# One product with the meta values for four frame tiles, in one PSUM bank, in a two-layer streaming encoder

## The chip, the cores and the metric

The kernel runs on one core of a Trainium2 chip. The metric is the device time of one execution in microseconds (us). The kernel before took 1335.31 us, the median of 3 runs (1331.56, 1336.21 and 1335.31).

Five engines work side by side, each on its own list of instructions: TensorE (PE, with its weight loads shown apart as PEld), VectorE (DVE), ScalarE (ACT), GpSimd (POOL), and SyncE (SP), which issues the transfers. Products are written to PSUM, which has eight banks of 512 float32 values on each of 128 partitions; ACT and DVE read them out of there.

## The reference, cut to what matters

Two layers over 592 tokens: 512 frames, 16 meta tokens ahead of them, and 64 sample tokens of another stream. Each layer makes one wide input projection, a recurrent branch, a differential attention branch with 8 heads, and two output projections. The attention of one head over the prompt, which is what the change touches, is:

```
s = einsum('bqhcd,bkhcd->bhcqk', q, k) * HEAD_DIM ** -0.5      # two maps, c = 0, 1
s = where(mask, s, -inf)                    # frames see the meta tokens and chunks up to their own
p = softmax(s, axis=-1)
attn = p[:, :, 0] - lam * p[:, :, 1]
o = einsum('bhqk,bkhe->bqhe', attn, v)      # v has 128 columns per head
o = rms_norm(o, subln_w) * (1 - lam_init)   # over the 128 columns of a head
```

The queries of the frames are four tiles of 128. Tile i sees the 16 meta tokens and the frame tiles 0 to i, so its output is `attn_meta(i) @ v_meta + sum over j <= i of attn(i, j) @ v(j)`. Sample and meta queries are a fifth tile of 80 rows.

## The kernel before, in words

**Projections.** Nearly all of PE's work is `dense` (L208): a block of 128 output columns over 592 tokens, in two halves of up to 296 tokens. Each half is 24 products (8 slices of the contraction, and for each hi*hi, hi*lo and lo*hi of a float32r split). The weights come by DMA (`stg`), ACT copies the high part (`wh`, L156) and DVE or POOL subtracts the low part (`wl`, L161). POOL does it in the step after three halves, (Z, 0), (Z, 1) and (A, 0) (`POOL_LO`, L43).

**What sets the order.** The order is written out by hand: no scheduler moves anything. For each of 8 heads the blocks A, B, V and Z (queries, keys, values, gate) are projected in turn. After each half `dense` runs, in this order: the deferred instructions (`flush`), the evacuation of the half, one `step()` of every active generator, and the next pieces of `wl` and `wh`. `head_steps` is such a generator; it begins after a head's Z block and does the attention of the head piecemeal between the halves of the next heads' blocks. So the four frame tiles of head h get their products while head h+1 is projected: tiles 3 and 2 after the second half of V (the V step below), tiles 1 and 0 after the first half of Z (the first Z step), the sample tile after the second half of Z (the second Z step), and the root of the norm on POOL after the first half of the A block that follows (L618 on).

**The products (`PV_step`).** For a frame tile, L541 multiplies PM, the transposed meta probabilities of all four tiles (16 meta rows of tile i at partitions 32i), with `vm[:, i]`, in which only the 16 rows of tile i are filled; L543 adds one product for each frame tile j up to i. All of them are float32 with 128 moving columns. Tiles 3 and 1 go to the bank `po`, tiles 2 and 0 to the bank `pt`. ACT copies each output to `oraw` (L550) and squares it with a running sum into a column of `ss` (L552). Each float32 product shows as two PE records, one for each of two weight loads; they are called passes here.

**What follows on the same engines.** In each step the same head's successor also runs its scores: in the V step and in the Z steps PE goes on with L476 and L479 into `pss`, DVE takes the row maximum (`nm`, L506), ACT the exponentials (`P`, L509), and then the next `wh`. At the next `flush` DVE combines the two maps (L483, L484 and `AT`, L489), and behind that stands the evacuation of the Z half (`zt` on DVE, L756, and `zg` on ACT, L757).

Of the kernel before, what the change touches and what calls it, by code (L numbers as in the profile page):

```python
# [22 lines left out]
FT = mybir.dt.float32  # L23
# [3 lines left out]
AF = mybir.ActivationFunctionType  # L27
# [60 lines left out]
def tile_kernel(ctx, tc, I, O):  # L88
    nc = tc.nc
    V, S, P, PE, SY = nc.vector, nc.scalar, nc.gpsimd, nc.tensor, nc.sync  # L90
    ctx.enter_context(tc.manual_schedule())

    def pool(name, **kw):
        return tc.tile_pool(name=name, bufs=1, reuse_waits="tile", **kw)
# [8 lines left out]
    def blk(name, dt=FT, w=T):  # L103

        return ar.tile([128, w], dt, name=name, tag="blk", bufs=ARENA)
# [4 lines left out]
    def ps_t():  # L110
        return ps.tile([128, 512], FT, name="pt")
# [4 lines left out]
    def ps_o():  # L116
        return ps.tile([128, 512], FT, name="po")
# [276 lines left out]
    po = ps_o()  # L394
# [15 lines left out]
    for k in range(KT):  # L410
# [6 lines left out]
        sq = acc0 if k == 0 else blk("sq")  # L417
# [3 lines left out]
        for n in range(2):  # L421
            for i, (a, b) in enumerate(((0, hwh), (0, hwl), (1, hwh))):
                for hf, (c0, m) in enumerate(ALL):
                    PE.matmul(banks[n][hf][:, :m], wt[n][a][:, k], b[k][:, c0:c0 + m], start=(k == 0 and i == 0),
                              stop=(k == KT - 1 and i == 2))
# [10 lines left out]
    def head_steps(l, h, at, shared, QF, KF, kcv, vT, gate, oa):  # L436
        AM, qlz, vt, vm = shared
# [30 lines left out]
        ss = at.tile([128, 5], FT, name="ss", bufs=2)  # L468
        P.memset(Z, 1.0)
        P.memset(ss, 1.0)  # L470
        AT, PT, pcs = {}, {}, {}
# [56 lines left out]
        def T_sample():  # L528
# [4 lines left out]
            PT[4] = at.tile([128, 3, 80], FT, name="PT4")  # L533
            S.activation(PT[4].rearrange("p a b -> p (a b)"), pa[:, :240], AF.Copy)

        def PV_step(i, p):
            nq = 128 if i < 4 else 80
            if i < 4:
                j0 = i * (i + 1) // 2
                o = p[:, :128]  # L540
                PE.matmul(o, PM, vm[:, i], start=True, stop=False)  # L541
                for j in range(i + 1):
                    PE.matmul(o, PT[0][:, j0 + j], vt[:, j], start=False, stop=(j == i))  # L543
            else:
                t = PT[4]
                for j in range(2):
                    PE.matmul(p[:nq, :128], t[:, j], cv[:, j], start=(j == 0), stop=False)
                PE.matmul(p[:nq, :128], t[:, 2], vt[:, 4], start=False, stop=True)

            S.activation(oraw[:nq, i], p[:nq, :128], AF.Copy)  # L550
            sq = at.tile([128, 128], FT, name="sq")
            S.activation(sq[:nq], oraw[:nq, i], AF.Square, accum_out=ss[:nq, i:i + 1])  # L552

        build(0)
        yield
# [33 lines left out]
        PM = at.tile([128, 128], FT, name="PM")  # L589
# [13 lines left out]
        yield  # L603
        oraw = at.tile([128, 5, 128], FT, name="oraw")
        P.memset(oraw[64:, 4], 0.0)
        PV_step(3, ps_o())
        PV_step(2, ps_t())
        yield
        PV_step(1, ps_o())
        PV_step(0, ps_t())  # L610
        yield
        PV_step(4, ps_t())
        rz0 = at.tile([128, 5], FT, name="rz0", bufs=2)
# [25 lines left out]
        o = oa[h] = blk("oa")  # L639
# [9 lines left out]
    def head(l, h, at, shared, hw, oa, hook, after):  # L649
# [96 lines left out]
        def evac_zs(hf, *x):  # L746
            evac_z(hf, *x)
            if hf == 1:
                active.append(head_steps(l, h, at, shared, QK[0], QK[1], kcv, vT, lambda: zg, oa))
# [78 lines left out]
    for l in range(DEPTH):  # L828
# [6 lines left out]
        at = ats.enter_context(pool(f"at{l}"))  # L835
# [3 lines left out]
        vt = at.tile([128, 5, 128], FT, name="vt")  # L839
        vm = at.tile([128, 4, 128], FT, name="vm")  # L840
# [21 lines left out]
        for nm in order_rnn():  # L862
            j = int(nm[2:])
# [50 lines left out]
            if rp is None and not active:  # L914
# [5 lines left out]
                    lambda n, dt, i=i: rp.tile([128, T], dt, name=f"{n}{i}") for i in range(3)]))  # L920
# [248 lines left out]
```

## Time and profile before

| | |
|---|---|
| median of 3 runs | 1335.31 us |
| the profiled execution | 1332.49 us, of which the span is 1330.6 us |
| PE busy | 1311.8 us (99%), 9768 records |
| DVE, ACT, POOL busy | 969.5 (73%), 674.0 (51%), 370.8 us (28%) |
| granted PE clock | 0.998 of full speed |
| DMA | 179.06 MB, mean 135 GB/s |

The span is the time from the first to the last instruction of the profiled execution; the 1.9 us around it are start and end. A busy share of 99% says that PE has almost always something under way; the ends of its records are modelled and overlap, so what one product takes of PE's time is read from start to start in the timeline. ACT's and POOL's busy time lies beside PE's, and counts only where PE waits for what they make.

### The profile page before, as it was taken

Reading aid. Unit: us, or ns where it says so; the run is one execution under the profiler, and the core shown is the slowest. Engines: PE = TensorE matmul, PEld = TensorE weight load, DVE = VectorE, ACT = ScalarE, POOL = GpSimd, SP = SyncE. Lnnn points to the kernel's source line nnn. Section 1 sums busy time; section 2 is a strip of 40 time slices with the busy share of each in tenths; the row PEclk is TensorE's granted clock in tenths of the full one; section 3 lists DMA queues with packets and bytes.
Section 4 is the critical chain, followed back from the end, with each engine's and each line's share of the span. In section 5 each row is a group of like instructions: output and inputs, shape, how many; then the busy total and the mean of one; then the engine's idle time right before and its main releaser. Section 6 shows DMA issues by size and latency. Waiting matters only on the chain.

```text
span 1330.6 us, 26310 instructions
## 1 busy us (share of the span) xinstructions
PE 1311.8 (99%) x9768; PEld 1305.4 (98%) x9768; DVE 969.5 (73%) x2031; ACT 674.0 (51%) x1575; POOL 370.8 (28%) x736
## 2 busy tenths in 40 slices
PE   8999999999999999999999999999999999999997
PEld 8999999999999999999999999999999999999997
DVE  6998888875467886555568888888734789855566
ACT  5465555564236674423425555555642566653343
POOL 1324544442212331000212344444331144200011
PEclk9999999999999999999999999999999999999999
DMA  6557777775332221223543677777653222222254
GB/s 227 170 139 182 179 169 181 180 168 146 98 110 86 73 84 64 97 80 116 179 143 112 168 187 178 177 180 185 161 155 106 85 76 88 80 80 80 90 184 139
DMA packets 260575, 179.06 MB, mean 135 GB/s; under 512 B 177952, under 2 KB 222624, under 8 KB 260448
## 3 DMA queue, kind: packets, MB, share of 16 engines
q1 hardware_dynamic: 260016, 176.85, 47.5%
q8 instruction: 77, 1.26, 0.4%
q14 instruction: 50, 0.41, 0.1%
q10 hardware_dynamic: 432, 0.53, 0.1%
HBM read 132.37 MB, written 35.26 MB: 126 GB/s over the span
## 4 chain that ended last, share of the span: by engine, by line
PE 79%; issue 7%; POOL 5%; DVE 3%; DMA 3%; ACT 1%; SPq 1%; ACTq 0%; POOLq 0%; DVEq 0%
PE pd L208 68%; PE pss L476 2%; PE pss L479 2%; PE pss L789 2%; PE po L543 2%; DMA stg<-in_w_dram 1%; PE pss L208 1%; PE pt L543 1%; POOL wl L161 1%; DMA gw<-in_gw_dram 1%; POOL ny L276 1%; POOL na L271 1%; DMA kcv<-in_cache_dram 1%; PE pt L541 1%; PE po L541 0%
## 5 line engine op out<-in xcount | busy, mean ns | idle before, releaser
L208 PE MATMUL pd<-hwh,wl 128*128 128x296 f32 (+1 forms) x1968 | 587.9, 299 | 6.0 <-POOL wl L161 5.3
L208 PE MATMUL pd<-hwh,wh 128*128 128x296 f32 (+1 forms) x1968 | 589.0, 299 | 0.4 <-DVE xs L662 0.4
L208 PE MATMUL pd<-hwl,wh 128*128 128x296 f32 (+1 forms) x1968 | 586.2, 298 | 0.0
L208 PEld LDWEIGHTS pd<-hwh,wl 128*128 128x128 f32 x1968 | 370.2, 188 | 8.4 <-POOL wl L161 7.2
L208 PEld LDWEIGHTS pd<-hwh,wh 128*128 128x128 f32 x1968 | 370.6, 188 | 0.7 <-DVE xs L662 0.5
L208 PEld LDWEIGHTS pd<-hwl,wh 128*128 128x128 f32 x1968 | 370.9, 188 | 0.0
L161 DVE TENSOR_TENSOR wl<-stg,wh 128x512 fp32r<-128x512 f32 x321 | 244.4, 765 | 0.3 <-ACT wh L156 0.2
L156 ACT ACTIVATE wh<-stg 128x512 fp32r<-128x512 f32 x364 | 221.7, 621 | 5.3 <-DVE wl L161 1.7
L509 ACT ACTIVATE P<-pss,nm 128x400 f32<-128x400 f32 (+4 forms) x128 | 62.5, 493 | 89.1 <-DVE nm L506 79.6
L674 POOL TENSOR_TENSOR xc<-xc,xr 128x592 f32<-128x592 f32 x32 | 48.1, 1502 | 212.0 <-DMA xr<-xs 124.8
L757 ACT ACTIVATE zg<-zt 128x296 f32<-128x296 f32 (+1 forms) x64 | 28.7, 449 | 154.2 <-DVE zt L756 147.8
L161 POOL TENSOR_TENSOR wl<-stg,wh 128x512 fp32r<-128x512 f32 x43 | 62.9, 1462 | 85.6 <-ACT wh L156 66.0
L208 PE MATMUL pd<-oah,wl 128*128 128x296 f32 (+1 forms) x256 | 76.4, 298 | 0.8 <-DVE wl L161 0.8
L208 PE MATMUL pd<-mh,wh 128*128 128x296 f32 (+2 forms) x256 | 77.0, 301 | 0.0
L208 PE MATMUL pd<-oal,wh 128*128 128x296 f32 (+1 forms) x256 | 76.2, 298 | 0.0
L208 PE MATMUL pd<-mh,wl 128*128 128x296 f32 (+2 forms) x256 | 76.2, 298 | 0.0
L208 PE MATMUL pd<-orl,wh 128*128 128x296 f32 (+1 forms) x256 | 76.1, 297 | 0.0
L208 PE MATMUL pd<-oah,wh 128*128 128x296 f32 (+1 forms) x256 | 76.1, 297 | 0.0
L208 PE MATMUL pd<-orh,wl 128*128 128x296 f32 (+1 forms) x256 | 76.0, 297 | 0.0
L208 PE MATMUL pd<-ml,wh 128*128 128x296 f32 (+2 forms) x256 | 75.9, 296 | 0.0
L208 PE MATMUL pd<-orh,wh 128*128 128x296 f32 (+1 forms) x256 | 75.9, 296 | 0.0
L756 DVE TENSOR_TENSOR zt<-pd,rb 128x288 f32<-128x288 f32 (+1 forms) x62 | 28.5, 460 | 43.7 <-PE pd L208 43.3
(257 smaller groups left out, 2521.5 us busy)
## 6 DMA issues: line engine op xcount, KB each, us to landing
stg<-in_w_dram SPq DMA_DIRECT2D x182, 512.0 KB, 3.9
pd<-AB SPq DMA_DIRECT2D x64, 160.0 KB, 3.7
PT<-pd SPq DMA_DIRECT2D x64, 160.0 KB, 3.5
xr<-xs SPq DMA_DIRECT2D x128, 74.0 KB, 5.0
od<-ob SPq DMA_DIRECT2D x64, 80.0 KB, 3.4
kv<-kv SPq DMA_DIRECT2D x64, 76.0 KB, 2.2
out_new_k_dram<-xc SPq DMA_DIRECT2D x16, 296.0 KB, 3.5
out_new_v_dram<-vT SPq DMA_DIRECT2D x16, 296.0 KB, 3.6
```

What stands on the lines that cost most here:

```text
L156: S.activation(hi, src, AF.Copy)
L161: E.tensor_tensor(lo, src, f32(hi), op=OP.subtract)
L208: PE.matmul(p[:, :m], a[:, k], b[k][:, c0:c0 + m], start=(i == 0), stop=(i == 23))
L271: E.tensor_tensor(a, a, b, op=OP.mult)
L476: PE.matmul(p[:nq, slot, :nn], qs[c][:, q0:q0 + nq], ks[c][:, k0:k0 + nn], start=True, stop=False)
L479: PE.matmul(p[:nq, slot, :nn], qlz[c][:, q0:q0 + nq], ks[c][:, k0:k0 + nn], start=False, stop=True)
L509: S.activation(pcs[i, cc][:nq, :n], p[:nq, cc, :n], AF.Exp, bias=nm[:nq, cc:cc + 1], accum_out=Z[:nq, cc, i:i + 1])
L543: PE.matmul(o, PT[0][:, j0 + j], vt[:, j], start=False, stop=(j == i))
L674: P.tensor_tensor(xc[x][:, :T], xc[x][:, :T], r[:, :T], op=OP.add)
L756: V.tensor_tensor(zt[:, cs], p[:, :m], rb[:, cs], op=OP.mult)
L757: S.activation(zg[:, cs], zt[:, cs], AF.Tanh, scale=0.5)
L789: PE.matmul(p[:, hf, :298], w[:, g], x[:, 298 * hf:298 * hf + 298], start=(i == 0), stop=(i == 2))
```

## The change

The product with the meta values is made once for all four tiles: 512 moving columns (`vm` as one row of 4 times 128), into the whole bank `po`. The frame products of tile i accumulate on columns 128i to 128i+127 of that bank. After tile 0, the last, one copy of 512 columns takes all four outputs to `oraw`, and the four squares follow one another. The sample tile is as before, but for the square, which is now in a function.

```
-                o = p[:, :128]
-                PE.matmul(o, PM, vm[:, i], start=True, stop=False)
+                o = p[:, 128 * i:128 * i + 128]
                 for j in range(i + 1):
-                    PE.matmul(o, PT[0][:, j0 + j], vt[:, j], start=False, stop=(j == i))
+                    PE.matmul(o, PT[0][:, j0 + j], vt[:, j], start=False, stop=(i == j == 0))
+                return
...
-        PV_step(3, ps_o())
-        PV_step(2, ps_t())
-        yield
-        PV_step(1, ps_o())
-        PV_step(0, ps_t())
+        po = ps_o()
+        PE.matmul(po, PM, vm.rearrange("p i e -> p (i e)"), start=True, stop=False)
+        PV_step(3, po)
+        PV_step(2, po)
+        yield
+        PV_step(1, po)
+        PV_step(0, po)
+        S.activation(oraw[:, 0:4].rearrange("p i e -> p (i e)"), po, AF.Copy)
+        for i in range(4):
+            squares(128, i)
         yield
```

`squares(nq, i)` is the old L552, with its tile `sq`. In the changed kernel the large product is L610, the frame products are L546, the large copy is L616 and the squares are L538.

On PE, in the V step of the second head (`hwh`, `hwl` and `wh`, `wl` are the two parts of the activations and the weights; lines with a space stand in both):

```order
 L208 MATMUL pd<-hwl,wh 128x296
 L208 MATMUL pd<-hwh,wl 128x296
-L541 MATMUL po<-vm,PM 128x128
-L543 MATMUL po<-vt,PT 128x128 x4
-L541 MATMUL pt<-vm,PM 128x128
-L543 MATMUL pt<-vt,PT 128x128 x3
+L610 MATMUL po<-vm,PM 128x512
+L546 MATMUL po<-vt,PT 128x128 x7
 L476 MATMUL pss<-ks_958,qs_960 128x272
 L479 MATMUL pss<-ks_958,qlz_346 128x272
```

Two products of 128 columns have gone from here, and the one of 512 has come. On PE in the first Z step of that head:

```order
 L208 MATMUL pd<-hwl,wh 128x296
 L208 MATMUL pd<-hwh,wl 128x296
-L541 MATMUL po<-vm,PM 128x128
-L543 MATMUL po<-vt,PT 128x128 x2
-L541 MATMUL pt<-vm,PM 128x128
-L543 MATMUL pt<-vt,PT 128x128
+L546 MATMUL po<-vt,PT 128x128 x3
 L476 MATMUL pss<-ks_958,qs_960 128x256
 L479 MATMUL pss<-ks_958,qlz_346 128x256
```

Here two products have gone and nothing has come. On ACT, the rows of before from the V step to the exponentials of the first Z step of the same head (`P,Z` are the exponentials and their sums):

```order
L550 ACTIVATE oraw<-pt 128x128
L552 ACTIVATE sq,ss<-oraw 128x128
L509 ACTIVATE P,Z<-pss,nm 128x272 x2
L156 ACTIVATE wh<-stg 128x512
L491 ACTIVATE AM<-AT 128x16
L757 ACTIVATE zg<-zt 128x296
L550 ACTIVATE oraw<-po 128x128
L552 ACTIVATE sq,ss<-oraw 128x128
L550 ACTIVATE oraw<-pt 128x128
L552 ACTIVATE sq,ss<-oraw 128x128
L509 ACTIVATE P,Z<-pss,nm 128x144 x2
L156 ACTIVATE wh<-stg 128x512
```

And the rows that stand there now:

```order
L509 ACTIVATE P,Z<-pss,nm 128x272 x2
L156 ACTIVATE wh<-stg 128x512
L491 ACTIVATE AM<-AT 128x16
L765 ACTIVATE zg<-zt 128x296
L616 ACTIVATE oraw<-po 128x512
L538 ACTIVATE sq,ss<-oraw 128x128 x4
L509 ACTIVATE P,Z<-pss,nm 128x144 x2
L156 ACTIVATE wh<-stg 128x512
```

The V step has lost two copies and two squares; in the first Z step two copies have become one of 512 columns, and four squares follow it instead of two, all ahead of the exponentials of 144 columns.

## Rows read from the trace of the kernel before

**Rows 1.** The page's part 1: busy us, share of the span, instructions.

```profile
PE 1311.8 (99%) x9768; PEld 1305.4 (98%) x9768; DVE 969.5 (73%) x2031; ACT 674.0 (51%) x1575; POOL 370.8 (28%) x736
```

**Rows 2.** Who waited for whom: engine, line, releaser: total us, times, longest.

```profile
PEld pd L208 <- POOL wl L161: 7.2, 8, 1.5
PE pd L208 <- POOL wl L161: 5.3, 8, 1.3
```

**Rows 3.** Groups by shape: PE's products with the meta values, count, busy us, mean ns, idle before.

```profile
L541 PE MATMUL pt<-vm,PM 128*128 128x128 f32 x64 | 12.4, 275 | 0.0
```

**Rows 4.** Timeline of PE in one V step: start, us, engine, line, operation.

```profile
89.90 0.38 PE L541 MATMUL po<-vm,PM 128*128 128x128 f32 x2
90.12 1.06 PE L543 MATMUL po<-vt,PT 128*128 128x128 f32 x8
91.01 0.39 PE L541 MATMUL pt<-vm,PM 128*128 128x128 f32 x2
...
91.83 0.37 PE L476 MATMUL pss<-ks,qs 128*128 128x272 f32 x1
```

**Rows 5.** Timeline of PE: weights of 80 columns; then one moving column.

```profile
100.57 0.60 PE L547 MATMUL pt<-kcv,PT 128*80 128x128 f32 x4
...
101.01 0.38 PE L548 MATMUL pt<-vt,PT 128*80 128x128 f32 x2
...
1301.30 0.36 PE L291 MATMUL pt<-ones,acc 128*128 128x1 f32 x2
1301.52 0.36 PE L291 MATMUL pt<-ones,sq 128*128 128x1 f32 x2
```

**Rows 6.** Timeline of PE: float32r products of 400 columns, and the next.

```profile
86.26 0.34 PE L476 MATMUL pss<-ks,qs 128*128 128x400 f32 x1
86.44 0.34 PE L479 MATMUL pss<-ks,qlz 128*128 128x400 f32 x1
```

**Rows 7.** Timeline of ACT: the one copy of 512 columns out of PSUM.

```profile
28.19 0.60 ACT L315 ACTIVATE rb<-pt 128x512 f32<-128x512 f32 x1 [5.24 <-PE pt L314]
28.68 0.23 ACT L316 ACTIVATE rb<-po 128x80 f32<-128x80 f32 x1
```

**Rows 8.** Timeline of ACT in a first Z step; in brackets the idle time before.

```profile
130.73 0.26 ACT L550 ACTIVATE oraw<-po 128x128 f32<-128x128 f32 x1
131.02 0.31 ACT L552 ACTIVATE sq<-oraw 128x128 f32<-128x128 f32 x1
...
131.33 0.26 ACT L550 ACTIVATE oraw<-pt 128x128 f32<-128x128 f32 x1
...
132.29 0.38 ACT L509 ACTIVATE P<-pss,nm 128x144 f32<-128x144 f32 x1 [0.26 <-DVE nm L506]
```

**Rows 9.** Timeline of DVE in the second Z step of the same head.

```profile
133.60 0.37 DVE L489 SCALAR_TENSOR_TENSOR AT<-P,rz 128x144 f32<-128x144 f32 x1
...
134.76 0.47 DVE L756 TENSOR_TENSOR zt<-pd,rb 128x296 f32<-128x296 f32 x1 [0.78 <-PE pd L208]
```

**Rows 10.** Timeline of POOL and PE in the steps that follow.

```profile
136.38 0.20 POOL L618 TENSOR_TENSOR vv<-ss,rz 128x5 f32<-128x5 f32 x1 [1.19 <-ACT sq L552]
...
143.88 1.71 POOL L161 TENSOR_TENSOR wl<-stg,wh 128x512 fp32r<-128x512 f32 x1
...
145.65 0.41 PE L208 MATMUL pd<-hwh,wl 128*128 128x296 f32 x1 [0.56 <-POOL wl L161]
```

**Rows 11.** The same places for a head of the second layer.

```profile
859.93 0.16 DVE L483 RECIPROCAL rz<-Z 128x1 f32<-128x1 f32 x1 [0.93 <-ACT P L509]
...
862.27 0.20 POOL L618 TENSOR_TENSOR vv<-ss,rz 128x5 f32<-128x5 f32 x1 [0.28 <-ACT sq L552]
...
871.37 0.41 PE L208 MATMUL pd<-hwh,wl 128*128 128x296 f32 x1 [1.30 <-POOL wl L161]
```

**Rows 12.** The same places for another head of the first layer.

```profile
204.31 0.47 DVE L756 TENSOR_TENSOR zt<-pd,rb 128x296 f32<-128x296 f32 x1 [0.21 <-PE pd L208]
...
215.11 0.40 PE L208 MATMUL pd<-hwh,wl 128*128 128x296 f32 x1 [0.46 <-POOL wl L161]
```

More of the change, by code (lines that the diff above doesn't have):

```diff
@@ L534, in T_sample, with squares @@
             S.activation(PT[4].rearrange("p a b -> p (a b)"), pa[:, :240], AF.Copy)
+        def squares(nq, i):
+            sq = at.tile([128, 128], FT, name="sq")
+            S.activation(sq[:nq], oraw[:nq, i], AF.Square, accum_out=ss[:nq, i:i + 1])
         def PV_step(i, p):
@@ L550, in PV_step @@
             S.activation(oraw[:nq, i], p[:nq, :128], AF.Copy)
-            sq = at.tile([128, 128], FT, name="sq")
-            S.activation(sq[:nq], oraw[:nq, i], AF.Square, accum_out=ss[:nq, i:i + 1])
+            squares(nq, i)
         build(0)
```

## The prediction, written before the changed kernel ran

> **What bounds the kernel now.** I read the busy shares first. PE is busy for 99% of the span [rows 1], so the time is PE's time: a change counts if it takes passes off PE or changes how long PE stands still. The view of waits comes second. The wait of PE that an attention step can reach is the one for POOL's `wl`, 5.3 us in 8 places [rows 2]. To see what feeds it, the timeline is followed backwards from one such place: PE stands for 0.56 us at 145.65 because POOL's `wl` began only at 143.88; ahead of it POOL worked through the norm of a finished head, which began at 136.38, released by ACT's square of the sample tile [rows 10]. That square stands behind `zt` and `zg` of the Z half, and `zt` stands on DVE behind the combination of the maps, which waits for ACT's exponentials of the first Z step. So there is one thin chain from the ACT queue, where the change puts its squares, to a stall of PE.
>
> **PE: removed and added.** The group of L541 has 64 records into `pt` [rows 3] and as many into `po`: 64 products of two passes, four products for each of 16 heads. From 89.90 to 91.01 PE starts ten passes [rows 4], 0.111 us each. Eight passes of a head go: 0.888 us. Two passes of 512 columns come. No row shows a float32 pass wider than 128 columns, so its price is bounded.
>
> Upper end: a pass is made of its moving columns and grows with them, 4 x 0.111 = 0.444 us; two are 0.888, and nothing is gained. Lower end: a pass of 128 columns takes 0.111 us only because its weights take as long to load, and 512 columns stream as the float32r rows do, 400 columns in 0.18 us from start to start [rows 6], so 0.23 for 512; a head gains 0.888 - 0.46 = 0.43 us, 16 heads 6.8 us.
>
> Two rows speak on this. With one moving column and 128 weight columns two passes take 0.22 us (1301.30 to 1301.52), so a weight load alone does cost 0.11. But with weights of 80 columns and 128 moving columns four passes take 0.44 us (100.57 to 101.01), again 0.11 each [rows 5]: 48 weight columns less shorten nothing, so there the moving columns are the limit. That row is the nearest in kind and I take the upper end, less the little of each pass that may not grow with columns: 0.01 us a pass, 0.02 us a head, -0.3 us in all.
>
> The Trainium skill has a rule that speaks for the lower end: "TensorE: Matmul & The Clock Gate", section Back-to-back issue gap, gives for a stream of loads and products 81 ns at 128 columns and 131 ns at 512. As an estimate from that page's ratio, a pass would go from 0.111 to 0.18 us, a head would gain 0.53 us and the kernel 8.5 us, against my 0.3. No row here shows such a stream in float32, and the row with 80 weight columns disagrees with what stands behind it, that the load sets the pace.
>
> The V step's block on PE becomes longer by 0.888 - 2 x 0.222 = 0.44 us, and the first Z step's shorter by 2 x 0.222 = 0.44 us. What PE does between them, one half of a projection, is later by 0.44 us, and back in place after it. Nothing of it is free or lost by itself.
>
> **ACT.** Four copies of 128 columns and four squares become one copy and four squares. In the V step ACT loses its two pairs, 2 x (0.29 + 0.31) = 1.2 us; the exponentials behind them wait for DVE's maximum, so nothing starts earlier. In the first Z step, before, two pairs run from 130.73 to 132.03, which is 132.29 less the 0.26 us of idle time [rows 8]. After: the copy starts 0.44 later with the shifted half, at 131.17; a copy of 512 columns takes 0.60 us [rows 7] and the square behind it can start some 0.02 after its end; four squares at 0.31 from start to start [rows 8] end at 131.17 + 0.62 + 1.24 = 133.03. The exponentials then start at 133.03 and not at 132.29, 0.74 us late. Queued behind them on ACT are `wh` and, on DVE, the combination of the maps.
>
> What hides it: DVE ends the combination at 133.60 + 0.37 = 133.97 and then waits 0.78 us for PE before `zt` [rows 9]. 0.74 us fits in by 0.04. POOL's `wl` of the second Z step, which waits for that `wh`, has 1.19 us of cover ahead of L618 [rows 10]. So for a head of this kind the square of the sample tile, L618 and the stall of PE stay as they are, give or take 0.1 us. Six of the eight places of [rows 2] are of this kind; I charge 0.07 us each, 0.4 us.
>
> Two of the eight have no such cover. In the second layer DVE waited 0.93 us for the exponentials themselves, and POOL's norm, at 862.27, had only 0.28 us idle before it; the stall is already 1.30 us [rows 11]. There ACT is not held by PE's half but by DVE's late `zt`, so the copy is not later, and only the longer queue counts: 0.62 + 1.24 - 1.30 = +0.56 us, which passes through to PE. In the first layer DVE's cover is 0.21 us [rows 12]; of 0.56 some 0.35 pass. Together +0.9 us. If in these two the half's delay of 0.44 came on top, it would be +0.9 more.
>
> **Other edits, at nothing.** `po` is held over one half of a projection instead of being emptied at once; its next user on PE, the transposes of the next sample tile, comes three halves after the copy, so the copy is long done. `pt` is used less. No DMA is added, dropped or moved on any queue. POOL reads `oraw` only after its norm. The products of tiles 1 and 0 no longer wait for copies of tiles 3 and 2, but that wait was empty. ACT's 674 us become some 7 us less (16 x (4 x 0.26 - 0.60)), beside PE.
>
> **Sum.** -0.3 + 0.4 + 0.9 = +1.0 us on the profiled execution's 1332.49: 1333.5 us. That execution lay 2.8 us below the median of the runs shown, and the runs spread over 4.7 us, so +1.0 us is not to be seen in them; on the median it would be 1336.3. I put the forecast between the two, at 1335.0 us. About 0.5%, 6.7 us, is what a measurement of this kernel can tell from no change.
>
> **Rivals.**
> 1. The wide pass is cheap. The mechanism is the lower end above: the moving stream at the speed of the float32r rows, and the 128-column passes held up by weight loads. For it: one moving column costs the same 0.11 us as 128. Against it: weights of 80 columns don't shorten a pass. Time: -6.8 + 1.3 = -5.5 us, 1327.0 on the profiled execution and 1329.8 on the median; about at the bound between faster and no change. Chance 0.10. The rule of the Trainium skill weighed above stands on this side.
> 2. ACT's queue passes through. The place is the first Z step, the price 0.74 us for each of the 8 stalls, 5.9 us, and with the 0.44 us of the shifted half on top up to 9.4 us. It decides from the point at which DVE's 0.78 us of cover is used up: an instruction of the combination that takes a few tenths longer, beside POOL's `wl`, is enough, since 0.04 us are left. For it: that cover is thinner in some heads, and the profile shows a head in which it is gone. Against it: it would need most of the eight at once. Time: 1332.49 - 0.3 + 5.9 to 9.4 = 1338.1 to 1341.6, on the median 1340.9 to 1344.4. Chance 0.13.
> 3. The relief of ACT is worth something. The copies of the V step are out of the way of `wh`, and the stalls shrink, at most by their whole 5.3 us: 1326.9 to 1332.2. Against it: none of the stalls waits for a `wh` of the V step. Chance 0.04, and near no change in its effect.
>
> **How the numbers follow.** The forecast has 0.73. Its own range is 1331 to 1339 with the spread of the runs. The range reaches down to most of rival 1, and up to the lower half of rival 2: 1328.5 to 1340.5. Faster by over 0.5% (below 1328.6): 0.09, nearly all of it rival 1. Slower by over 0.5% (above 1342.0): 0.11, the upper half of rival 2 and what I have not thought of. Within: 0.80.
>
> **What would show it.** On PE in the V step, the time from the start of L610 to that of the first L546 should be near 0.87 us; 0.46 would be rival 1. PE's block in the first Z step should be 0.67 us from L546 to L476. On ACT the exponentials of 144 columns should stand 0.7 us later behind `zt` than before, with no idle time ahead of them. DVE's wait ahead of the second `zt` should shrink from 0.78 to nearly 0; if it is gone and `zt` is late, rival 2 begins. PE's wait for POOL's `wl` should be 5.5 to 7.5 us in about 8 places; above 11 rival 2 has come, below 4 rival 3. The prediction would be wrong in its base if another wait of PE above 2 us appeared, or if a record showed L610 as more than two passes a head.

## The result, and the profile after

The changed kernel takes 1343.1 us (median of 6 runs, 1338.99 to 1349.41); the kernel before, in the same runs, 1332.84 us (6 runs). The ratio is 1.0078, with a 95% interval of 1.0061 to 1.0095: slower by 0.8%, against a forecast of no change. The profiled execution took 1349.41 us with a span of 1347.5 us, 16.9 us more than the profiled one of before; it is the longest of the six, and the terms below are read from it, not from a median run. Of the runs behind the experiments two were far longer at a low clock (1587.84 us at 0.751 with ACT's part alone, 1406.96 us at 0.85 with the squares moved); the medians below hold them, the ratios do not.

Part 1 of the page of the changed kernel, answering to [rows 1], and from its view of waits the row that answers to [rows 2] (total us, times, longest):

```profile
PE 1318.9 (98%) x9672; PEld 1304.4 (97%) x9672; DVE 960.5 (71%) x2031; ACT 668.1 (50%) x1527; POOL 373.4 (28%) x736
```

```profile
PE pd L208 <- POOL wl L161: 15.6, 10, 3.1
```

PE's wait for POOL's `wl` went from 5.3 us in 8 places to 15.6 us in 10: +10.3 us. Most of the rest of the 16.9 us is in the granted clock. Before, it was 1.00 in every stretch of 4 us until PE's work ended. After, it fell in six (columns: us, PE busy and records, granted clock, DMA share, GB/s):

```profile
148.00:152.00 4.00, 2.86 (x12) 0.51 0.99 223
152.00:156.00 4.00, 4.00 (x22) 0.64 0.84 236
776.00:780.00 4.00, 1.06 (x6) 0.94 1.00 147
780.00:784.00 4.00, 4.00 (x22) 0.63 0.85 258
884.00:888.00 4.00, 2.08 (x8) 0.67 0.96 159
888.00:892.00 4.00, 4.00 (x30) 0.91 0.90 257
```

0.51 is about the lower of the clock's two levels, 1.2 of 2.4 GHz. Each fall begins in or just behind one of the three longest stalls of PE, 3.03, 3.08 and 3.04 us, which ended at 149.14, 778.94 and 885.92. What the falls cost is read from the end of a stall to the start of L610 in the next head: 15.55, 14.52 and 14.25 us behind these three, and 13.0 behind the seven shorter stalls (111.93 to 124.95, for one). That is 5.3 us. With the 10.3 us of waiting it makes 15.6 of the 16.9; the other 1.3 us lie in pieces of some tenths, and nothing here shows what they are. The runs differ in the clock too: the six have mean clocks of 0.993, 0.994, 0.996, 0.996, 0.997 and 0.997, from the longest to the shortest.

PE's own part came as forecast. The timeline of PE in the V step of [rows 4]:

```profile
89.58 1.02 PE L610 MATMUL po<-vm,PM 128*128 128x512 f32 x2
90.44 1.73 PE L546 MATMUL po<-vt,PT 128*128 128x128 f32 x14
91.92 0.37 PE L476 MATMUL pss<-ks,qs 128*128 128x272 f32 x1
```

The two wide passes take 0.86 us (89.58 to 90.44), where 0.87 was written; the eight passes that went took 0.888. A wide float32 pass grows with its columns.

Two kinds of head are told apart below. In a common head the first `zt` stands 6.3 to 6.4 us behind L610, where PE allows it; in the other kind it is late. This is ACT's first Z step in a common head, answering to [rows 8], and DVE, POOL and PE behind it, answering to [rows 9, 10]:

```profile
172.54 0.31 ACT L538 ACTIVATE sq<-oraw 128x128 f32<-128x128 f32 x1
172.98 0.31 ACT L538 ACTIVATE sq<-oraw 128x128 f32<-128x128 f32 x1
173.41 0.31 ACT L538 ACTIVATE sq<-oraw 128x128 f32<-128x128 f32 x1
...
174.16 0.36 ACT L509 ACTIVATE P<-pss,nm 128x144 f32<-128x144 f32 x1
...
175.46 0.37 DVE L489 SCALAR_TENSOR_TENSOR AT<-P,rz 128x144 f32<-128x144 f32 x1
175.74 0.46 DVE L764 TENSOR_TENSOR zt<-pd,rb 128x296 f32<-128x296 f32 x1
...
177.36 0.52 POOL L626 TENSOR_TENSOR vv<-ss,rz 128x5 f32<-128x5 f32 x1 [0.31 <-ACT sq L538]
...
185.18 1.70 POOL L161 TENSOR_TENSOR wl<-stg,wh 128x512 fp32r<-128x512 f32 x1
...
186.93 0.40 PE L208 MATMUL pd<-hwh,wl 128*128 128x296 f32 x1 [1.13 <-POOL wl L161]
```

Three things are to be seen. The squares stand about 0.435 us apart, not 0.31. DVE's 0.78 us of waiting ahead of `zt` is gone. And from the norm's start to `wl` it is now 7.82 us (177.36 to 185.18), where the same head had 7.41 before. The stall is 1.13 us; it was 0.43.

DVE's wait is gone everywhere: in the ten heads that stall, the second `zt` now stands 4.65 to 4.72 us behind the first, without a wait for PE. ACT's queue sets it. Before, PE set it in seven of the eight that stalled; only in the head of [rows 11] did the queue, 3.62 us behind the first. So now every first `zt` that is late makes the second one late by as much.

The long stalls come in the other kind of head. Here is one, the same as in [rows 11], with POOL and DVE in the V step ahead of it and at the end of the norm:

```profile
866.19 1.46 POOL L682 TENSOR_TENSOR xc<-xc,xr 128x592 f32<-128x592 f32 x1 [7.18 <-DMA xr<-xs]
...
866.84 1.37 DVE L161 TENSOR_TENSOR wl<-stg,wh 128x512 fp32r<-128x512 f32 x1
...
868.09 1.28 POOL L161 TENSOR_TENSOR wl<-stg,wh 128x512 fp32r<-128x512 f32 x1 [0.17 <-ACT AM L491]
...
868.32 1.07 DVE L484 SCALAR_TENSOR_TENSOR rz<-rz,lm,Z 128x1 f32<-128x1 f32 x1
...
869.84 0.45 DVE L764 TENSOR_TENSOR zt<-pd,rb 128x288 f32<-128x288 f32 x1
...
876.10 0.39 POOL L626 TENSOR_TENSOR vv<-ss,rz 128x5 f32<-128x5 f32 x1 [0.28 <-ACT sq L538]
...
880.90 0.20 POOL L270 TENSOR_TENSOR na<-ny 128x5 f32<-128x5 f32 x1
881.03 0.77 DVE L462 TENSOR_TENSOR ks<-xc,ks 64x592 fp32r<-64x592 f32 x1
881.18 0.67 POOL L271 TENSOR_TENSOR na<-na,nb 128x5 f32<-128x5 f32 x1
881.83 0.77 DVE L463 SCALAR_TENSOR_TENSOR qlz<-xc,qs 64x592 fp32r<-64x592 f32 x1
881.94 0.75 POOL L275 TENSOR_SCALAR na<-na 128x5 f32<-128x5 f32 x1
...
884.04 1.82 POOL L161 TENSOR_TENSOR wl<-stg,wh 128x512 fp32r<-128x512 f32 x1
...
885.92 0.62 PE L208 MATMUL pd<-hwh,wl 128*128 128x296 f32 x1 [3.04 <-POOL wl L161]
```

The rotated keys (`xr`, by DMA) came late here, so POOL added them (`xc`) 4.0 us after the V step's first product, L610 at 862.18, beside DVE's `wl`, and POOL's own `wl` fell on DVE's combination: one value per partition took 1.07 us at 868.32, where 0.22 is usual. The first `zt` is 7.66 us behind that product, where PE alone would allow 6.3. So the head is late before ACT's queue begins, as it was before the change, and the whole of that queue's growth comes on top. The norm then runs later into DVE's work on the next head: POOL's instructions on five values take 0.67 and 0.75 us beside DVE's of 0.77, and 0.20 otherwise. The Trainium skill, "SBUF — State Buffer", section Terms, has VectorE and GpSimd share one pair of ports, held for a whole instruction while the other is blocked; these rows agree.

The sum over heads: of +10.3 us, the four heads with late keys, in which POOL's addition began 3.6 us or more behind L610 (stalls ending at 111.93, 149.14, 778.94 and 885.92) have +8.5, three common heads of the first layer +1.95 (+0.70, +0.66, +0.59), and three of the second layer -0.1.

### The profile page after: what moved, and what is told of

It is laid out like the page before. It is cut to its first block, busy times and chain, and to the rows that moved or that the text cites. A ratio compares the mean times of both kernels' runs of the same rounds, so it can differ in the third digit from the quotient of the medians.

```text
span 1347.5 us, 26124 instructions
## 1 busy us (share of the span) xinstructions
PE 1318.9 (98%) x9672; PEld 1304.4 (97%) x9672; DVE 960.5 (71%) x2031; ACT 668.1 (50%) x1527; POOL 373.4 (28%) x736
## 3 DMA queue, kind: packets, MB, share of 16 engines
q8 instruction: 76, 1.25, 0.4%
## 4 chain that ended last, share of the span: by engine, by line
PE 70%; issue 8%; POOL 7%; DVE 6%; DMA 4%; ACT 3%; SPq 2%; ACTq 0%; POOLq 0%; DVEq 0%
PE pd L208 60%; PE po L546 2%; PE pss L797 2%; DMA xr<-xs 1%; POOL wl L161 1%; PE pss L476 1%; PE pss L479 1%; ACT sq L538 1%; PE pss L208 1%; DVE wl L161 1%; DMA stg<-in_w_dram 1%; POOL na L275 1%; POOL ny L276 1%; PE po L610 1%; POOL na L270 1%
## 5 line engine op out<-in xcount | busy, mean ns | idle before, releaser
L208 PE MATMUL pd<-hwh,wl 128*128 128x296 f32 (+1 forms) x1968 | 591.1, 300 | 16.3 <-POOL wl L161 15.6
L161 DVE TENSOR_TENSOR wl<-stg,wh 128x512 fp32r<-128x512 f32 x321 | 237.1, 742 | 0.3 <-ACT wh L156 0.2
L518 ACT ACTIVATE P<-pss,nm 128x528 f32<-128x528 f32 x32 | 22.5, 702 | 90.5 <-DVE nm L516 65.5
```

The costliest lines, as they stand in the source:

```text
L161: E.tensor_tensor(lo, src, f32(hi), op=OP.subtract)
L208: PE.matmul(p[:, :m], a[:, k], b[k][:, c0:c0 + m], start=(i == 0), stop=(i == 23))
L518: S.activation(pcs[i, c][:, :528].rearrange("p (a b) -> p a b", a=2), p[:, :, :264], AF.Exp, bias=nm[:, :1], accum_out=Z[:, c, i:i + 1])
```

## The experiments

The theories were A, that the queue on ACT and the shift of PE's half add up against DVE's cover (the 0.78 us that DVE waited), and its rivals B, the shift alone, C, ACT's queue alone, and later D, that part of the loss does not go through PE's wait for POOL's `wl`. Times are medians; ratios are to the kernel before, in the runs of the same batch.

**PE's shift alone.**

```
-                PE.matmul(o, PM, vm[:, i], start=True, stop=False)
+                for _ in range({3: 3, 2: 1, 1: 0, 0: 0}[i]):
+                    PE.matmul(o, PM, vm[:, i], start=True, stop=True)
...
+                    PE.matmul(o, PT[0][:, j0 + j], vt[:, j], start=(j == 0), stop=(j == i))
```

> The kernel before, with only PE's part of the change: tile 3 makes its product with the meta values three times in the V step (two of them overwritten), tiles 1 and 0 leave theirs out, so the meta part of their output is missing. PE's block is 0.44 us longer in the V step and 0.44 us shorter in the first Z step, as in the changed kernel; ACT's list is that of before. Theory A (the queue on ACT and the shift of PE's half add up, and only what exceeds DVE's cover of 0.78 us reaches PE): the shift alone, 0.44, stays under the cover, so the time is that of before, 1330 to 1336 us, and PE waits 5 to 8 us for POOL's wl. Rival B (the shift alone does it, because DVE and POOL then collide otherwise in the V step): 1339 to 1347 us and over 12 us of that wait. Rival C (ACT's queue alone does it): as before.

Measured: 1333.43 us, ratio 1.0006 (0.9992 to 1.0019). The row of PE's wait:

```profile
PE pd L208 <- POOL wl L161: 4.5, 8, 0.7
```

No loss: rival B falls. This profile happens to have no long stall, not even the 1.30 us of [rows 11].

**ACT's part alone.**

```
-        PE.matmul(po, PM, vm.rearrange("p i e -> p (i e)"), start=True, stop=False)
...
+                PE.matmul(o, PM, vm[:, i], start=True, stop=False)
```

> The changed kernel with four products of 128 columns with the meta values, where they were before, still into one bank and out of it by one copy: ACT's part of the change alone. ACT's copy and four squares take 0.62 + 4 x 0.435 = 2.36 us in the first Z step instead of 1.30, so the exponentials are 1.06 us later behind the same PE. DVE's maximum hides 0.26 of it. Theory A: 0.80 against a cover of 0.78, so the common heads lose about nothing and the two without cover about 1 us each: 1333 to 1337 us, wait of PE for POOL's wl 6 to 9 us. Rival B: as before, 1330 to 1336, wait 5 to 6. Rival C: as the changed kernel, 1339 to 1347 us, wait 13 to 17.

Measured: 1343.83 us, ratio 1.0058 (1.0038 to 1.0077), wait 12.1 us in 10 places. The time is that of rival C, and A's number was wrong; the wait is a little under the 13 us of C. A common head and one with late keys, exponentials on ACT and stalls of PE:

```profile
137.25 0.37 ACT L509 ACTIVATE P<-pss,nm 128x144 f32<-128x144 f32 x1
...
149.59 0.40 PE L208 MATMUL pd<-hwh,wl 128*128 128x296 f32 x1 [0.55 <-POOL wl L161]
...
868.91 0.36 ACT L509 ACTIVATE P<-pss,nm 128x144 f32<-128x144 f32 x1
...
881.93 0.61 PE L208 MATMUL pd<-hwh,wl 128*128 128x296 f32 x1 [2.92 <-POOL wl L161]
```

The common head stalls 0.55 us, as before the change (0.56 in [rows 10]): there the cover holds, as A has it. All that the wait has grown by is in four heads with late keys, 2.12, 1.09, 2.46 and 2.92 us, and the clock fell behind three of these. So queue and shift add up only in the common heads; in the late ones the queue is enough.

**The squares behind the exponentials.**

```
         for i in range(4):
-            squares(128, i)
+            later(lambda i=i: squares(128, i))
```

> The changed kernel with the four squares moved behind the exponentials and the weights' high part of the first Z step, into the time in which ACT waits for the second Z half. Work on every engine is that of the changed kernel. Theory A: ACT's queue ahead of the exponentials is 0.62 us instead of 1.30, with the shift of 0.44 they are 0.25 us early, so PE's wait for POOL's wl is back at 4 to 7 us and the time at 1329 to 1336 us. Rival B (the shift): unchanged at 1339 to 1347. Rival C: as A. If the squares then hold up the second zg, the wait stays over 8 us.

Measured: 1338.01 us, ratio 1.0034 (1.0022 to 1.0046), wait 11.2 us. Half of the loss is gone, not all. In a common head the exponentials wait for DVE again and the stall is 0.55 us; in one with late keys the squares now stand in front of the second `zg`:

```profile
135.25 0.38 ACT L509 ACTIVATE P<-pss,nm 128x144 f32<-128x144 f32 x1 [0.51 <-DVE nm L506]
...
148.58 0.40 PE L208 MATMUL pd<-hwh,wl 128*128 128x296 f32 x1 [0.55 <-POOL wl L161]
...
900.45 0.31 ACT L538 ACTIVATE sq<-oraw 128x128 f32<-128x128 f32 x1
900.75 0.43 ACT L765 ACTIVATE zg<-zt 128x288 f32<-128x288 f32 x1
...
911.69 0.40 PE L208 MATMUL pd<-hwh,wl 128*128 128x296 f32 x1 [2.12 <-POOL wl L161]
```

There is no idle time ahead of `zg` at 900.75, and the norm is late by way of it. So the place in the queue is the cause in the common heads; the late heads have room for the squares in neither place.

**Four buffers for the squares' tile.**

```
-            sq = at.tile([128, 128], FT, name="sq")
+            sq = at.tile([128, 128], FT, name="sq", bufs=4)
```

> The changed kernel with four buffers for the tile that the squares write. It tells why four squares in a row stand 0.435 us apart where a copy stood 0.31 us behind a square. If the common output tile holds them up: 0.31 to 0.37 us apart, the queue 0.3 to 0.5 us shorter, and by theory A a wait for POOL's wl of 8 to 12 us and a time of 1335 to 1340 us. If it is the running sum that is read out after each square: 0.435 us still, and time and wait as in the changed kernel, 1339 to 1347 us and 13 to 17 us.

Measured: 1343.17 us, ratio 1.0076 (1.0055 to 1.0097), wait 11.8 us in 9 places. The squares:

```profile
134.27 0.31 ACT L538 ACTIVATE sq<-oraw 128x128 f32<-128x128 f32 x1
134.58 0.29 ACT L538 ACTIVATE sq<-oraw 128x128 f32<-128x128 f32 x1
```

0.30 us apart: the common output tile held them up, 0.13 us each. The time was not the forecast 1335 to 1340: the common heads stall 0.47 to 0.70 us again, but three heads with late keys still 1.81, 2.85 and 1.95 us, and the clock is 0.992 to 0.995 in these runs. A fourth head stalls long with keys that came only 1.95 us behind L610:

```profile
823.94 1.45 POOL L682 TENSOR_TENSOR xc<-xc,xr 128x592 f32<-128x592 f32 x1 [5.83 <-DMA xr<-xs]
824.02 1.81 DVE L489 SCALAR_TENSOR_TENSOR AT<-P,rz 128x400 f32<-128x400 f32 x1
...
844.85 0.40 PE L208 MATMUL pd<-hwh,wl 128*128 128x296 f32 x1 [2.23 <-POOL wl L161]
```

POOL's addition fell on DVE's combination of the maps, which took 1.81 us; at the same place in the first profile it took 0.64. Its first `zt` is 7.21 us behind L610. So late keys are one way to a late first `zt`, and not the only one.

**POOL's norm half a projection later, after and before.**

```
+        yield
         v = at.tile([128, 5], FT, name="vv", bufs=2)
         P.tensor_tensor(v, ss, rz0, op=OP.mult)
```

One empty step behind it goes, and `Z` and `ss` have three buffers.

> The changed kernel with POOL's norm of a head one projection half later (one of the empty steps behind it taken out, so what follows stays where it was), so POOL's wl after the first A half no longer stands behind the norm. Theory A now: ACT's queue makes the norm late, most in the heads whose first zt is late already, the late norm makes wl late, PE stalls, and after some of the long stalls its clock is low for a while. All of the loss goes through that one wait, so it goes here: wait of PE for POOL's wl under 2 us, granted clock 0.998, time 1326 to 1331 us and within 0.2% of the kernel before with the same edit. Rival D: part of the 10 us is lost elsewhere, on PE or in DVE and POOL holding each other up: over 4 us above the kernel before with the same edit.

> The kernel before with POOL's norm one projection half later: the control for the run with the same edit of the changed kernel. Its 5.3 us of PE's wait for POOL's wl go: 1326 to 1330 us, by both theories.

Measured: 1328.86 us (0.9967, 0.9956 to 0.9979) with the change, 1325.56 us (0.9942, 0.9918 to 0.9965) without it. The wait for POOL's `wl` is gone in both. The 10 us between the two kernels become 3.3, more than the 0.2% that A gave; another wait of PE has come with the change, for the DVE instruction that empties a PSUM bank:

```profile
PE pd L208 <- DVE xs L670: 3.0, 3, 1.4
```

Without the change it is 0.3 us. The control came out just under its forecast of 1326. So this pair leaves it open whether all the loss goes through the one wait.

**DVE makes that `wl`, after and before.**

```
-POOL_LO = {("Z", 0), ("Z", 1), ("A", 0)}
+POOL_LO = {("Z", 0), ("Z", 1)}
```

> The changed kernel with the wl of the first A half subtracted on DVE instead of POOL, the norm where it was: another way to take the norm out of PE's way, at the price of 0.75 us more work of DVE per head. Theory A: PE's wait for POOL's wl is gone; if DVE keeps up, 1326 to 1333 us and within 0.3% of the kernel before with that edit. If DVE becomes late in its place, PE waits for DVE's wl by more than 2 us, and the times of both are up. Rival D: over 4 us above the kernel before with that edit.

> The kernel before with the wl of the first A half on DVE: the control. 1326 to 1333 us by both theories, unless DVE becomes late.

Measured: 1326.01 us (0.9945, 0.9923 to 0.9966) with the change, 1324.73 us (0.9935, 0.9915 to 0.9954) without it, again just under its forecast. The first row of PE's waits with the change:

```profile
PE pd L208 <- DVE wl L161: 1.4, 4, 0.4
```

It was 1.5 us before the change as well. Without the one wait the change costs 1.3 us, a tenth of a per cent, and the granted clock is 0.997 to 0.998. That settles it: nearly all of the 10 us goes through POOL's `wl` of the first A half. Rival D falls. Both kernels beat the two of the case.

**The change by pairs: products of 256 columns, copies of 256.**

```
+                if i % 2:
+                    PE.matmul(p[:, :256], PM, vm[:, i - 1:i + 1].rearrange("p i e -> p (i e)"), start=True, stop=False)
...
+                if i % 2 == 0:
+                    S.activation(oraw[:, i:i + 2].rearrange("p i e -> p (i e)"), p[:, :256], AF.Copy)
```

> The change by pairs: in each of the two steps one product of 256 columns for two tiles into one bank, one copy of 256 columns and two squares. PE's blocks and ACT's queue are then as long as before (copy of 256 about 0.37, two squares at 0.435: 1.24 us against 1.30), only with two products of 256 columns instead of four of 128. Theory A: as before, 1331 to 1336 us and 4 to 8 us of PE's wait for POOL's wl, and no gain on PE. A theory that merging itself (one bank for several tiles, wide products) costs: over 1338 us. If wide float32 passes were cheap: under 1329 us.

Measured: 1333.35 us, ratio 1.0000 (0.9990 to 1.0009). PE in a V step, a head with late keys, and the wait:

```profile
123.71 0.59 PE L542 MATMUL po<-vm,PM 128*128 128x256 f32 x2
124.14 1.73 PE L544 MATMUL po<-vt,PT 128*128 128x128 f32 x14
...
784.00 1.46 POOL L683 TENSOR_TENSOR xc<-xc,xr 128x592 f32<-128x592 f32 x1 [6.84 <-DMA xr<-xs]
...
801.70 0.40 PE L208 MATMUL pd<-hwh,wl 128*128 128x296 f32 x1 [0.71 <-POOL wl L161]
```

```profile
PE pd L208 <- POOL wl L161: 4.7, 8, 0.7
```

Merging is not what costs. With ACT's queue as long as before, keys that come 3.6 us behind the V step's first product (780.36 to 784.00) do no harm: the stall is 0.71 us. (In the kernel before, keys that came 4.1 us behind it went with the 1.30 us of [rows 11].) Two passes of 256 columns take 0.43 us.

**Four buffers and DVE's `wl` together.**

```
-POOL_LO = {("Z", 0), ("Z", 1), ("A", 0)}
+POOL_LO = {("Z", 0), ("Z", 1)}
...
+            sq = at.tile([128, 128], FT, name="sq", bufs=4)
```

> The changed kernel with four buffers for the squares' tile and the wl of the first A half on DVE: the best form of the change. Theory A: the wait is gone whatever ACT's queue, so as the changed kernel with DVE's wl alone, 1324 to 1327 us, and not clearly under the kernel before with DVE's wl (1324.7), since the wide product saves PE 0.3 us.

Measured: 1323.94 us, ratio 0.9927 (0.9912 to 0.9942). It is the fastest of all, but not told apart from the kernel before with DVE's `wl` (0.9915 to 0.9954).

**The changed kernel once more.**

> The changed kernel once more, for a second profile. If the transfer of the rotated keys sets which heads have a late first zt, the heads with the long stalls (149, 779 and 886 us in the first profile) are others this time, or as many at other places, each with POOL's addition xc starting 3.5 us or more behind the V step's products; heads with an early xc stall 0.5 to 1.2 us again. If the place in the program sets it, the same heads stall.

Measured: 1349.46 us, wait 16.6 us in 10 places. A head with late keys that was not one in the first profile, and the next, which was:

```profile
827.54 1.47 POOL L682 TENSOR_TENSOR xc<-xc,xr 128x592 f32<-128x592 f32 x1 [6.89 <-DMA xr<-xs]
...
847.33 0.40 PE L208 MATMUL pd<-hwh,wl 128*128 128x296 f32 x1 [2.78 <-POOL wl L161]
...
861.15 1.62 POOL L682 TENSOR_TENSOR xc<-xc,xr 128x592 f32<-128x592 f32 x1 [6.50 <-DMA xr<-xs]
...
883.13 0.40 PE L208 MATMUL pd<-hwh,wl 128*128 128x296 f32 x1 [0.59 <-POOL wl L161]
```

The first is 3.7 us behind its V step's product at 823.81, the second 0.7 us ahead of the one at 861.84. The head that stalled 3.04 us in the first profile stalls 0.59 us in this one. So the place in the program does not decide which heads stall long; in these two profiles they are the heads with late keys. No run moved the keys alone.

## Why the prediction was wrong

**What bounds the kernel: right.** The chain from ACT's queue by way of `zt`, the second square and POOL's norm to PE's wait for `wl` is the one that carried the loss, and with that wait taken away nearly nothing of the loss is left (1326.01 against 1324.73 us). By the prediction's own sign, over 11 us of that wait, rival 2 had come (15.6).

**PE removed and added: right.** -0.3 us was written; 16 x (0.86 - 0.888) is -0.4. Rival 1 fell: passes of 128, 256 and 512 columns take 0.111, 0.215 and 0.43 us. The ratio of 131 to 81 ns that the Trainium skill gives ("TensorE: Matmul & The Clock Gate", section Back-to-back issue gap) does not hold for these passes: 0.43 to 0.111 us is near to four.

**ACT: the mechanism right, the term too small.** The step that failed first is "four squares at 0.31 from start to start". The row showed a copy 0.31 us behind a square; a square behind a square that writes the same tile is 0.435. The queue is 0.62 + 4 x 0.435 = 2.36 us and not 1.86. With that, the margin of 0.04 us in DVE's cover is overdrawn. The common heads of the first layer lost about 0.65 us each where 0.07 was charged. Only some 0.15 of it is the later start of the norm (12.67 us behind L610, and 12.52 behind L541 before); 0.41 is the norm itself, which ran longer beside DVE's instructions, a term that the prediction did not have. The second layer's lost nothing, as their norm became shorter by what it was later. And this term is not what put the time out of the range: with the squares at 0.30, as priced, the common heads lost nothing and the median was 1343.17 us all the same.

**"Two of the eight have no such cover", +0.9 us: the step that carried the loss.** In the profiled execution it should have been +8.5. I took the head of [rows 11] as a property of that head and priced it at the queue's growth alone. It is a state into which a head can come, in this profile by a late transfer of its keys; there were four of them in the profile after, and two of them stood at places that had not stalled at all. The other head that was named, that of [rows 12], became a common one and lost 0.66. And each lost more than the queue: for the head of [rows 11], 1.30 to 3.04 us, of which 1.0 is the later start of the norm (13.92 us behind the V step's first product, and 12.91 before), 0.6 the longer norm beside DVE's work (7.94, and 7.34 before), and 0.1 the `wl` itself.

**The clock: not thought of.** The prediction put it at nothing without a word. The granted clock fell with the three stalls of 3 us, and that cost 5.3 us in the profiled execution.

**The rivals and the range.** What came is rival 2 in its mechanism, at a chance of 0.13; its 1340.9 to 1344.4 us on the median holds the time, though not in the heads that it named, and not without the clock; that its numbers fit is in part luck. The range ended at 1340.5, below the lower bound of that.

**What stays open.** The falls of the clock went with stalls of 1.95 us and more, but not with each: the execution with the squares moved has a stall of 2.70 us and a mean clock of 0.998. What decides it the runs don't show. Nor was it shown what delays the keys' transfers, or where the rest of the difference with the late norm comes from. How the 10.3 us of the medians divide between waiting and clock is not known either, as only the longest run was profiled, and one more like it.

## What to carry to other kernels

Merging small copies into a large one takes work off an engine and still lengthens the queue at one place, because all that hung on the pieces moves behind the last of them; price it by what stands right behind, and by how two instructions of one kind follow each other, not by a row in which they alternate with others. A cover that a margin of hundredths holds is to be priced as lost, and a bad head in a profile as a state that others can fall into. Where PE waits for a product of an engine that has other work ahead of it, making that product elsewhere was worth 0.6% here, more than the 5.5 us that the most hopeful rival gave the change.

## What the runs showed of the hardware that was not expected

- Four squares with a running sum stand 0.435 us apart on ACT when they write one tile, 0.30 us with four tiles.
- With a stall of PE of 3 us the granted clock can fall to about half for some 3 to 7 us; in one execution three such stalls were followed by a loss of 2.5, 1.5 and 1.25 us.
- A float32 product's pass takes 0.111, 0.215 and 0.43 us for 128, 256 and 512 moving columns.
- DVE's float32 instructions on SBUF and POOL's hold each other up: 0.22 became 1.07 us and 0.64 became 1.81 us on DVE, 0.20 became 0.75 on POOL.
